# Issuing a pair's gate products before attention opens, a longer head norm in the issue model, and one tile of queries for the row scores

## The chip, the cores and the metric

One Trainium2 chip, one core. The metric is the device time of one execution in microseconds. Five engines are named throughout: PE (TensorE, matrix products, with PEld for its weight loads), DVE (VectorE), ACT (ScalarE), POOL (GpSimd) and SP (SyncE, which here only issues transfers). Each engine works through its own list of instructions in order and waits on semaphores for the others.

## The reference

One layer of a diffusion backbone. A normalised and modulated input goes through one projection `w_in`, whose columns feed a Fourier group and an attention group; both are gated by a SiLU and joined in one output projection:

```python
xn = _rms_norm(x, norm_g) * (1 + sc_x) + sh_x           # x: 1024 x 1024
fx_in, fx_gate, qx, kx, vx, nx_gate = split(xn @ w_in)   # 512 columns each
qx, kx = _rms_norm(heads(qx), q_norm_g), _rms_norm(heads(kx), k_norm_g)   # 8 heads of 64
f_out = fourier(fx_in, w_four) * silu(fx_gate)
s_loc = q . k over a 2-D neighbourhood, * 64 ** -0.5, + relative bias, masked
s_ctx = q . k over all 256 context tokens, * 64 ** -0.5
p = softmax(concat(s_loc, s_ctx))
na_out = (p_loc . v + p_ctx . v_ctx) * silu(nx_gate)
out = x + g_x * (concat(f_out, na_out) @ w_out)
```

Everything is float32.

## The kernel before

**Numbers.** Most products use a number format of PE with fewer mantissa bits (`R`). To keep float32's accuracy each operand is split in a high part and a low part, and three products (high by high, high by low, low by high) are summed. A split is a cast by ACT (`act.copy` into an `R` tile) and a subtraction by DVE or POOL (`tensor_tensor`, L198 or L110).

**Stages.** From 0 to some 128 us come the norm, the Fourier gate and the first part of the Fourier transform. Then one large stage runs, in which the projection, the context and the attention are interleaved, until some 498 us; after it stand the output products. Attention works on the eight heads as four pairs p of two heads h. For each pair:

- `project` (L810 on): eight row tiles t; for each, 24 products of 384 columns (`pqkv`, queries, keys and values of the pair at once), ACT copies the result to `raw`, and `head_norm` (L723 on) scales queries and keys: ACT squares, DVE sums (L729, L730), POOL takes the power -0.5 (`hrs`, L733), DVE multiplies (`raw`, L734).
- `gate_proj` (L843 on): 48 products of 512 columns (`png`), then ACT and DVE make the gate (L854, L855).
- `queries` (L898 on) and `keys`, each for two halves q of the 1024 rows: PE transposes four tiles of `raw` into a bank (`ptq`, L903; `ptk`, L917); ACT and DVE write high and low parts.
- `row_max` (L1158 on), once for each head and row tile: four score products (`s`, L1171 and L1173), DVE adds the bias and takes the maximum (`pr`, L1179), ACT the exponential (L1183).
- `probs` (L1240 on), twelve steps a head: PE transposes `pr` into a bank (`st`), ACT and DVE split it (`eh`, `el`), PE multiplies by the values (`pv`).

The last pair has the output products of the Fourier half (`po`, L1447) as its filler, and the splitting of their weights (`owr`, `oh`, `ol`) and inputs (`mh`, `ml`) beside it.

**How the scores keep the low parts.** Of a head h, `a` is its half of the 128 partitions (`HALF[h]`) and `b` the other. `qs1[h]` holds the high part of the transposed queries in `a` and the low part in `b`. `ks1[h]` holds the high part of the keys in `a` and again in `b`; `ks2[h]` their low part in `a` and zeros in `b`. So `qs1` by `ks1` is high by high plus low by high, in one product over 128 partitions. The missing high by low comes from `qs2[h]` (the high part copied to `a`, zeros in `b`) by `ks2[h]`.

**What sets the order.** The program writes each engine's list itself (`manual_schedule`). A small model of the engines runs while the program is built: `chain` hands each operation to an engine with a duration in us (`a_t`, `d_t`, `p_t` or a number), and an operation is written on its engine's list when the model says that it is free and the inputs are ready. PE's list is made from a set of generators, asked in turn (`seq_build`, `seq_rows`, `seq_scores` and others); only if none of them has work does `run_fill` take the next product of `feed`, which is the projection, then the gate products, then the output products. So a wrong duration costs no time in the model, but puts work on a list too early or too late. Operations with two possible engines (`split_by`, `copy_by`) go to the one that is free first in the model. `open_attention` (L963 on) allocates the attention's tiles, once the context is done; it lets POOL clear tiles and DVE build small constants, and counts that with `OP` us for POOL and `OD` us for DVE. `seq_build` calls it before the first `queries`. `PRB` and `EHB` are numbers of buffers for `pr` and for `eh` and `el`.

Of the kernel before, what the change touches and what calls it, by code (L numbers as in the profile page):

```python
# [26 lines left out]
AHEAD, GAINS = 2, ((0,), (1, 2), (3, 4), (5, 6), (7,), (), (), ())  # L27
S = dict(sem=0.13, rw=4, wo=2.6, rt=0, ri=12, rf=0, ro=1, ns=3, rr=2, rv=2)
WHO = dict(ml=(1, 0), ol=(0, 1), w=None, cw=(0, 1), ga=None, ce=(1, 0), el=(0,), vl=(0, 1), q2=(0,), kb=(0, 2), fm=None, wc=(2,), ec=(2,), oc=(0, 2), mc=(2, 0), cc=(2, 0), vc=(2,), fe=(0,), gc=(2,))
OP, OD, OC = 4.5, 2.0, 8.0  # L30
SEQ = 1024
CTX = 256
NB = 8
# [9 lines left out]
def tile_hybrid_block(  # L43
# [140 lines left out]
    def a_t(n):  # L184
        return 0.09 + n * 0.00083
# [624 lines left out]
    def project(p):  # L810
        raws[p] = []
        for t in range(NB):
            while now[0] < banks[0]:
                yield None
            if t % 4 == 0:
                while p and not has(("v", p - 1, 0, t // 4), ("v", p - 1, 1, t // 4)):
                    yield None
                raw = rawp.tile([P, 4, 384], F32, tag="raw", name="raw")
                raws[p].append(raw)
            o = pj("pqkv")[:, 0:384]  # L820
            ts_ = slice(t * P, (t + 1) * P)
            for k in range(KT):
                while ("w", p, k) not in done:
                    yield None
                wh, wl = weights[p][k]
                for n, (x, w) in enumerate(((xnh, wh), (xnh, wl), (xnl, wh))):
                    mm(o, x[k][:, ts_], w, start=(k == 0 and n == 0), stop=(k == KT - 1 and n == 2))  # L827
                    yield 0.16
                if t == NB - 1 and p < 3:
                    prep(p + 1, k)  # L830
            rt = raw[:, t % 4]
            sqt = rawp.tile([P, 256], F32, tag="sqt", name="sqt")
            while t > 1 and ("raw", p, t - 2) not in done:
                yield None
            banks.append(1e9)
            banks.pop(0)
            n1, n2, n3, n4 = head_norm(rt[:, 0:256], sqt, 4)
            chain((ACT_, a_t(384), lambda rt=rt, o=o: act.copy(rt, o), 0),  # L838
                  lambda: banks.__setitem__(0 if banks[0] == 1e9 else 1, clock()),
                  (ACT_, a_t(256), n1), (DVE_, 0.42, n2), (POOL_, 0.96, n3), (DVE_, d_t(256), n4),  # L840
                  lambda t=t: done.__setitem__(("raw", p, t), 1), rank=S["rr"])

    def gate_proj(p):  # L843
# [54 lines left out]
    def queries(p, q):  # L898
        cs = slice(512 * q, 512 * q + 512)
        tbs[0] -= 1  # L900
        pq = tb("ptq")
        for j in range(4):
            pe.transpose(pq[:, j * P:(j + 1) * P], raws[p][q][:, j, 0:P], ident)  # L903
        for h in range(2):
            a, b = HALF[h], HALF[1 - h]
            chain((ACT_, a_t(512), lambda h=h, a=a: act.copy(qs1[h][a, cs], pq[a])),
                  (DVE_, d_t(512), lambda h=h, a=a, b=b: dve.tensor_tensor(out=qs1[h][b, cs], in0=pq[a], in1=f(qs1[h][a, cs]), op=ALU.subtract)),
                  lambda h=h: give() if h else None,
                  copy_by(512, WHO["q2"], qs2[h][a, cs], f(qs1[h][a, cs])),
                  lambda h=h: done.__setitem__(("q", p, h, q), 1), rank=h)  # L910

    def keys(p, c, cs, srcs):
# [44 lines left out]


    gts, att = ExitStack(), ExitStack()
    gtp = ap1 = ap2 = qs1 = qs2 = ks1 = ks2 = eye = rrow = sel = biases = trs = sms = None  # L960
    PRB, VSB = 5, 1

    def open_attention():  # L963
        nonlocal gtp, ap1, ap2, qs1, qs2, ks1, ks2, eye, rrow, sel, biases, trs, sms
        gfs.close()
        pqs.close()
        gst.close()
        gtp = gts.enter_context(tc.tile_pool(name="gtp", bufs=1, **LT))
        ap1 = att.enter_context(tc.tile_pool(name="ap1", bufs=1, **LT))
        ap2 = att.enter_context(tc.tile_pool(name="ap2", bufs=2, **LT))  # L970
        qs1 = [ap1.tile([P, SEQ], R, name=f"qs1{h}") for h in range(2)]
        qs2 = [ap1.tile([P, SEQ], R, name=f"qs2{h}") for h in range(2)]
        ks1 = [ap1.tile([P, SEQ + CTX], R, name=f"ks1{h}") for h in range(2)]
        ks2 = [ap1.tile([P, SEQ + CTX], R, name=f"ks2{h}") for h in range(2)]
        for h in range(2):
            b = HALF[1 - h]
            pool.memset(f(qs2[h])[b], 0.0)
            pool.memset(f(ks2[h])[b], 0.0)
        eye = ap1.tile([104, 8], F32, name="eye")
        dve.tensor_copy(eye, ident[0:104, 0:8])  # L980
        for r in (32, 64, 96):
            dve.tensor_copy(eye[r:r + 8], ident[0:8, 0:8])
        rrow = [ap1.tile([104, P], R, name=f"rrow{n}") for n in range(2)]
        for r in rrow:
            dve.memset(f(r), 0.0)
        half = ap1.tile([104, 2], F32, name="half")
        sel = [ap1.tile([104, P], R, name=f"sel{z}") for z in range(2)]
        for z in range(2):
            dve.reduce_sum(half[:, z:z + 1], eye[:, 4 * z:4 * z + 4], axis=AX.X)
            dve.memset(f(sel[z]), 0.0)  # L990
            for h in range(2):
                r = slice(64 * h, 64 * h + 40)
                dve.tensor_copy(sel[z][r, HALF[h]], half[r, z:z + 1].broadcast_to([40, 64]))
        dve.tensor_tensor(out=eye[:, 0:4], in0=eye[:, 0:4], in1=eye[:, 4:8], op=ALU.add)
        biases = [ap1.tile([P, 896], F32, name=f"bias{n}") for n in range(2)]
        for b in biases:
            pool.memset(b[:, 256:512], 0.0)
        trs = [ap1.tile([P, 40], F32, name=f"tr{h}") for h in range(2)]
        sms = [ap1.tile([P, 8], F32, name=f"sm{h}") for h in range(2)]
        for h in range(2):  # L1000
            pool.memset(trs[h], 0.0)
        free[POOL_] = max(free[POOL_], now[0]) + OP
        free[DVE_] = max(free[DVE_], now[0]) + OD
        for e in (POOL_, DVE_):
            at(free[e], lambda e=e: issue(e))
        done["open"] = 1
# [151 lines left out]
    def row_max(p, h, t):  # L1158
# [8 lines left out]
        for z in range(2):  # L1167
            for o, kk in ((sl, lk), (sc, slice(SEQ, SEQ + CTX))):
                st, sp = (z == 0 and not (edge and o is sc)), (z == 1 and not (edge and o is sl))
                if z == 0:  # L1170
                    mm(o, qs1[h][:, ts_], ks1[h][:, kk], start=st, stop=sp)  # L1171
                else:
                    mm(o, qs2[h][:, ts_], ks2[h][:, kk], start=st, stop=sp)  # L1173
        now[0] += 2 * (nl + CTX) / 2400
        done["s", p, h, t] = 1
        pr = prs[p, h, t] = ap1.tile([P, 640], F32, tag="pr", bufs=PRB, name="pr")[:, 0:nl + CTX]
# [41 lines left out]


    STEPS = (10, 11, 0, 1, 2, 3, 12, 4, 13, 5, 6, 7)  # L1220
    EHB = 3
    pvs = {}

    def turned(p, h, t, kt):
# [324 lines left out]
    def feed():  # L1549
# [3 lines left out]
        for p in range(4):  # L1553
            yield from project(p)
            if p == 3:
                wst.close()
                yield from gate_rows()
                side.append(out_loads())
            while "open" not in done:
                yield None  # L1560
            yield from gate_proj(p)
            if p < 3:
                prep_gate(p + 1)
# [192 lines left out]
```

## Time and profile before

| | |
|---|---|
| three runs, us | 574.51, 576.97, 578.93 |
| median, us | 576.97 |
| profiled execution, us | 575.37 |
| its span, first to last instruction, us | 573.6 |
| PE, DVE, ACT, POOL busy, share of the span | 95%, 68%, 55%, 24% |
| granted PE clock, mean | 0.997 of 2.4 GHz |

A row of the timeline gives the start in us from the first instruction, the duration, the engine, the source line, the operation, what it writes and reads, and how many like it were merged; in brackets stands how long the engine was idle before it and what ended that. A product's recorded duration overlaps the next one's, so what a product costs is read from the distance between starts, or from the chain of work, which counts each moment once.

### The profile page before, as it was taken

Reading aid. Unit: us, or ns where it says so; the run is one execution under the profiler, and the core shown is the slowest. Engines: PE = TensorE matmul, PEld = TensorE weight load, DVE = VectorE, ACT = ScalarE, POOL = GpSimd, SP = SyncE. Lnnn points to the kernel's source line nnn. Section 1 sums busy time; section 2 is a strip of 40 time slices with the busy share of each in tenths; the row PEclk is TensorE's granted clock in tenths of the full one; section 3 lists DMA queues with packets and bytes.
Section 4 is the critical chain, followed back from the end, with each engine's and each line's share of the span. In section 5 each row is a group of like instructions: output and inputs, shape, how many; then the busy total and the mean of one; then the engine's idle time right before and its main releaser. Section 6 shows DMA issues by size and latency. Waiting matters only on the chain.

```text
span 573.6 us, 9000 instructions
## 1 busy us (share of the span) xinstructions
PE 546.6 (95%) x3299; PEld 483.5 (84%) x3299; DVE 388.5 (68%) x801; ACT 312.6 (55%) x662; POOL 139.9 (24%) x144
## 2 busy tenths in 40 slices
PE   4899999999999899999999999999999898989997
PEld 3677896799878889999989999899998687868886
DVE  5774756686754868866678667777765978783142
ACT  6865462355665368764688646767456855520000
POOL 2200000115702533112431032411224513540000
PEclk9999999999999899999999999999999999999999
DMA  8991046426551521110221111220113556120052
GB/s 339 412 408 58 1 148 215 152 89 198 193 147 38 179 65 42 42 43 37 81 66 45 30 49 51 70 70 1 42 46 112 184 191 203 73 92 0 1 201 93
DMA packets 41459, 64.64 MB, mean 113 GB/s; under 512 B 3268, under 2 KB 25156, under 8 KB 40392
## 3 DMA queue, kind: packets, MB, share of 16 engines
q1 hardware_dynamic: 40408, 60.40, 31.1%
q0 software_dynamic: 1008, 3.67, 1.9%
q8 instruction: 26, 0.43, 0.3%
q14 instruction: 17, 0.14, 0.1%
HBM read 55.15 MB, written 8.91 MB: 112 GB/s over the span
## 4 chain that ended last, share of the span: by engine, by line
PE 75%; DVE 8%; ACT 6%; DMA 6%; issue 2%; POOL 2%; SPq 1%; POOLq 0%; DVEq 0%; ACTq 0%
PE pqkv L827 20%; PE of L1623 8%; PE pg L365 7%; PE po L1447 5%; PE st L1251 4%; PE png L849 4%; DMA wr<-in_w_in_dram 3%; PE s L1171 2%; PE s L1173 2%; PE pv L1285 2%; PE pv L1275 2%; DMA x<-in_xb_dram 2%; DMA owr<-in_w_out_dram 2%; PE pc L1133 1%; PE pw L502 1%
## 5 line engine op out<-in xcount | busy, mean ns | idle before, releaser
L827 PE MATMUL pqkv<-wl,xnh 128*128 128x384 f32 x256 | 88.3, 345 | 0.0
L827 PE MATMUL pqkv<-wh,xnl 128*128 128x384 f32 x256 | 88.0, 344 | 0.0
L827 PE MATMUL pqkv<-wh,xnh 128*128 128x384 f32 x256 | 87.8, 343 | 0.0
L733 POOL TENSOR_TENSOR hrs<-hss,mhalf 128x4 f32<-128x4 f32 (+1 forms) x34 | 36.7, 1082 | 149.2 <-DVE hss L730 145.8
L1262 DVE TENSOR_TENSOR el<-st,eh 128x512 fp32r<-128x512 f32 (+2 forms) x96 | 53.5, 572 | 17.0 <-ACT eh L1261 16.3
L1261 ACT CAST eh<-st 128x512 fp32r<-128x512 f32 (+2 forms) x96 | 47.0, 494 | 29.4 <-PE st L1251 25.9
L1183 ACT ACTIVATE pr<-pr,tr 128x640 f32<-128x640 f32 (+1 forms) x64 | 51.5, 805 | 15.4 <-DVE tr L1179 15.1
L1179 DVE CUSTOM_DVE_ANT_0 pr<-s,bias 128x640 f32<-128x640 f32 (+1 forms) x64 | 50.2, 784 | 10.6 <-PE s L1173 10.2
L827 PEld LDWEIGHTS pqkv<-wh,xnh 128*128 128x128 f32 x256 | 48.7, 190 | 0.6
L827 PEld LDWEIGHTS pqkv<-wl,xnh 128*128 128x128 f32 x256 | 48.6, 190 | 0.5
L827 PEld LDWEIGHTS pqkv<-wh,xnl 128*128 128x128 f32 x256 | 48.6, 190 | 0.4
L1251 PE MATMUL st<-ident,pr 128*128 128x128 f32 x304 | 47.3, 272 | 0.1
L1251 PEld LDWEIGHTS st<-ident,pr 128*128 128x128 f32 x304 | 37.0, 140 | 2.8 <-DVE el L1262 0.5
L1447 PE MATMUL po<-oh,mh 128*128 128x512 f32 x88 | 31.0, 396 | 3.0 <-DVE y L1453 1.5
L1627 DVE TENSOR_TENSOR y<-y,of 128x512 f32<-128x512 f32 (+1 forms) x17 | 11.1, 656 | 32.3 <-PE of L1623 32.3
L1171 PE MATMUL s<-ks,qs 128*128 128x256 f32 (+1 forms) x128 | 29.9, 313 | 0.7 <-DVE tr L1179 0.7
L203 ACT CAST wh<-wr 128x384 fp32r<-128x384 f32 (+1 forms) x44 | 22.6, 539 | 12.7 <-DMA wr<-in_w_in_dram 10.6
L1173 PE MATMUL s<-ks,qs 128*128 128x256 f32 (+1 forms) x128 | 28.3, 302 | 0.0
L198 DVE TENSOR_TENSOR wl<-wr,wh 128x384 fp32r<-128x384 f32 (+1 forms) x29 | 21.5, 754 | 9.6 <-ACT wh L203 7.7
L198 POOL TENSOR_TENSOR wl<-wr,wh 128x384 fp32r<-128x384 f32 (+1 forms) x19 | 20.9, 1104 | 28.9 <-ACT wh L203 15.2
L365 PE MATMUL pg<-xnh,w 128*128 128x512 f32 x96 | 27.3, 406 | 0.0
L838 ACT COPY raw<-pqkv 128x384 f32<-128x384 f32 x32 | 15.3, 478 | 21.4 <-PE pqkv L827 21.1
(295 smaller groups left out, 1442.9 us busy)
## 6 DMA issues: line engine op xcount, KB each, us to landing
wd<-in_w_ada_b_dram SPq DMA_DIRECT2D x8, 1024.0 KB, 11.6
wr<-in_w_in_dram SPq DMA_DIRECT2D x40, 192.0 KB, 2.8
wr<-in_w_in_dram SPq DMA_DIRECT2D x24, 256.0 KB, 3.1
x<-in_xb_dram SPq DMA_DIRECT2D x8, 512.0 KB, 7.3
wdg<-in_w_ada_g_dram SPq DMA_DIRECT2D x8, 512.0 KB, 4.7
owr<-in_w_out_dram SPq DMA_DIRECT2D x16, 256.0 KB, 3.4
y<-in_xb_dram SPq DMA_DIRECT2D x8, 512.0 KB, 5.4
out_dram<-y SPq DMA_DIRECT2D x15, 256.0 KB, 2.1
```

The source lines that it names most:

```text
L198: return [(e, time(n), lambda eng=eng: eng.tensor_tensor(out=out, in0=in0, in1=in1, op=op)) for e, eng, time in (both[k] for k in who)]
L365: mm(pg[j][hf], wj, x[i][:, hs], start=(i == 0 and g == 0), stop=(i == KT - 1 and g == 2))
L827: mm(o, x[k][:, ts_], w, start=(k == 0 and n == 0), stop=(k == KT - 1 and n == 2))
L1171: mm(o, qs1[h][:, ts_], ks1[h][:, kk], start=st, stop=sp)
L1173: mm(o, qs2[h][:, ts_], ks2[h][:, kk], start=st, stop=sp)
L1179: dve.tensor_tensor_reduce(out=pr, in0=sv, in1=bt, scale=-1.0, scalar=3.0e38, op0=ALU.add, op1=ALU.min, accum_out=tr[:, t:t + 1])
L1183: (ACT_, a_t(nl + CTX) + 0.15, lambda: act.activation(pr, pr, AF.Exp, bias=tr[:, t:t + 1], scale=-1.0, accum_out=sm[:, t:t + 1]), 1),
L1251: pe.transpose(s[:, j * P:(j + 1) * P], turned(p, h, t, kt), ident)
L1261: chain((ACT_, a_t(m), lambda: act.copy(eh[:, w], s3)), (DVE_, d_t(m), lambda: dve.tensor_tensor(out=el[:, w], in0=s3, in1=f(eh)[:, w], op ...
L1262: (DVE_, d_t(m), lambda: dve.tensor_tensor(out=el[:, w], in0=s3, in1=f(eh)[:, w], op=ALU.subtract)), give,
L1447: mm(o, mf[k][m][:, ts_], wf[hf][k][w_], start=(k == 0 and n == 0), stop=(k == 3 and n == 2))
L1623: mm(o[:, cs], ma[k][m][:, ts_], w[:, cs], start=(k == 0 and n == 0), stop=(k == 3 and n == 2))
```

## The change

Five edits. (1) `feed` no longer waits for `open_attention` before the gate products of a pair. (2) In `project` the model's duration of POOL's power goes from 0.96 to 1.1 us and that of DVE's multiplication from 0.34 (`d_t(256)`) to 0.9 us. (3) The second score products read `qs1` instead of `qs2`: `ks2` is zero in `b`, so the low part of the queries that stands there in `qs1` is multiplied by zero. `qs2`, its sixteen copies and its two clearings go. (4) `PRB` goes from 5 to 6 and `EHB` from 3 to 4. (5) `OP` goes from 4.5 to 3.5 us.

```diff
-OP, OD, OC = 4.5, 2.0, 8.0
+OP, OD, OC = 3.5, 2.0, 8.0
@@ project
-                  (ACT_, a_t(256), n1), (DVE_, 0.42, n2), (POOL_, 0.96, n3), (DVE_, d_t(256), n4),
+                  (ACT_, a_t(256), n1), (DVE_, 0.42, n2), (POOL_, 1.1, n3), (DVE_, 0.9, n4),
@@ queries
                   lambda h=h: give() if h else None,
-                  copy_by(512, WHO["q2"], qs2[h][a, cs], f(qs1[h][a, cs])),
                   lambda h=h: done.__setitem__(("q", p, h, q), 1), rank=h)
@@
-    PRB, VSB = 5, 1
+    PRB, VSB = 6, 1
@@ open_attention
-        qs2 = [ap1.tile([P, SEQ], R, name=f"qs2{h}") for h in range(2)]
...
-            pool.memset(f(qs2[h])[b], 0.0)
             pool.memset(f(ks2[h])[b], 0.0)
@@ row_max
-                if z == 0:
-                    mm(o, qs1[h][:, ts_], ks1[h][:, kk], start=st, stop=sp)
-                else:
-                    mm(o, qs2[h][:, ts_], ks2[h][:, kk], start=st, stop=sp)
+                mm(o, qs1[h][:, ts_], (ks1, ks2)[z][h][:, kk], start=st, stop=sp)
@@
-    EHB = 3
+    EHB = 4
@@ feed
-            while "open" not in done:
-                yield None
             yield from gate_proj(p)
```

The edits move rows on all engines. On POOL, at the opening of attention (`hrs` is the power of the head norm, `bias` and `tr` are tiles of the row scores), before:

```order
L733 TENSOR_TENSOR hrs<-hss,mhalf 128x4
L977 MEMSET qs_2102 64x1024
L978 MEMSET ks_2106 64x1280
L977 MEMSET qs_2103 64x1024
L978 MEMSET ks_2107 64x1280
L997 MEMSET bias_2133 128x256
L997 MEMSET bias_2134 128x256
```

and now:

```order
L733 TENSOR_TENSOR hrs<-hss,mhalf 128x4
L975 MEMSET ks_2104 64x1280
L975 MEMSET ks_2105 64x1280
L994 MEMSET bias_2129 128x256
L994 MEMSET bias_2130 128x256
```

The two clearings of `qs2` are gone and the rest follows sooner. DVE's list at the same place keeps its order. On PE, at the first transposes of the queries (first pair, first half), before:

```order
L827 MATMUL pqkv<-wh,xnh_406 128x384
L827 MATMUL pqkv<-wl,xnh_406 128x384
L827 MATMUL pqkv<-wh,xnl_410 128x384
L903 MATMUL ptq<-ident,raw 128x128 x4
L917 MATMUL ptk<-ident,raw 128x128 x4
```

and now:

```order
L827 MATMUL pqkv<-wh,xnh_406 128x384
L827 MATMUL pqkv<-wl,xnh_406 128x384
L827 MATMUL pqkv<-wh,xnl_410 128x384
L827 MATMUL pqkv<-wh,xnh_407 128x384
L827 MATMUL pqkv<-wl,xnh_407 128x384
L827 MATMUL pqkv<-wh,xnl_411 128x384
L903 MATMUL ptq<-ident,raw 128x128 x4
L916 MATMUL ptk<-ident,raw 128x128 x4
```

Three projection products have moved ahead of the transposes. In both kernels 51 more of them follow, then the context's key transposes and, before, six projection products (now three), and only then the first gate product. On PE, at the second half's transposes in the last pair (`pgr` turns the output gate's column into rows), before:

```order
L827 MATMUL pqkv<-wh,xnl_413 128x384
L1380 MATMUL pgr<-ident,gcol 128x128 x8
L849 MATMUL png<-xnh_121,gh 128x512
L849 MATMUL png<-xnl_125,gh 128x512
L849 MATMUL png<-xnh_121,gl 128x512
L903 MATMUL ptq<-ident,raw 128x128 x4
```

and now:

```order
L827 MATMUL pqkv<-wh,xnl_413 128x384
L1374 MATMUL pgr<-ident,gcol 128x128 x8
L849 MATMUL png<-xnh_121,gh 128x512
L849 MATMUL png<-xnl_125,gh 128x512
L849 MATMUL png<-xnh_121,gl 128x512
L849 MATMUL png<-xnh_121,gh 128x512
L849 MATMUL png<-xnl_125,gh 128x512
L849 MATMUL png<-xnh_121,gl 128x512
L849 MATMUL png<-xnh_122,gh 128x512
L903 MATMUL ptq<-ident,raw 128x128 x4
```

Four gate products have moved ahead of the transposes. At the same half in the first pair 18 gate products stand ahead of `ptq` where 15 stood. In the last pair, between these transposes and the end of attention, DVE's list loses two casts of `qs`, one split of context values, two of values and one of a mix tile (`ml`), and gains two casts and two splits of output weights; POOL's changes the other way for the splits. On SP three loads change places with a neighbour: a bias tile with a weight tile, `y1` with a bias tile, `y6` with an output weight.

## Rows read from the trace of the kernel before

**Rows 1.** The page: span, and PE's busy time, share, instructions.

```profile
span 573.6 us, 9000 instructions
PE 546.6 (95%) x3299; PEld 483.5 (84%) x3299; DVE 388.5 (68%) x801; ACT 312.6 (55%) x662; POOL 139.9 (24%) x144
```

**Rows 2.** Stretches: length, each engine's busy time (instructions), granted clock, DMA share, GB/s.

```profile
190.00:200.00 10.00, 7.63 (x38) 7.36 (x37) 7.92 (x23) 3.77 (x7) 4.09 (x8) 0.83 0.58 165
200.00:430.00 230.00, 229.04 (x1458) 218.57 (x1457) 170.90 (x384) 153.25 (x345) 59.76 (x64) 1.00 0.16 49
430.00:507.00 77.00, 69.58 (x402) 59.29 (x400) 62.14 (x113) 46.17 (x92) 30.83 (x22) 1.00 0.42 146
...
194.30:197.70 3.40, 3.40 (x14) 3.40 (x13) 2.58 (x7) 1.85 (x3) 1.01 (x1) 0.50 0.53 146
440.00:460.00 20.00, 16.97 (x93) 13.81 (x93) 18.79 (x32) 16.70 (x34) 10.38 (x7) 1.00 0.53 185
```

**Rows 3.** Waits of PE: who for whom, us in total, times, longest.

```profile
PE ptq L903 <- DVE raw L734: 3.8, 2, 2.4
PE pv L1275 <- DVE el L1262: 2.9, 4, 1.2
```

**Rows 4.** Timeline of PE at the first transposes of the queries.

```profile
191.19 0.49 PE L903 MATMUL ptq<-ident,raw 128*128 128x128 f32 x3
194.05 0.33 PE L903 MATMUL ptq<-ident,raw 128*128 128x128 f32 x1 [2.37 <-DVE raw L734]
195.31 0.52 PE L827 MATMUL pqkv<-wl,xnh 128*128 128x384 f32 x1
```

**Rows 5.** The chain that ended last: start, us, engine, what, how many.

```profile
188.19 2.10 DVE eye L982
190.30 0.99 DVE eye L982
...
280.91 2.43 PE pqkv L827 x14
283.34 3.91 PE png L849 x17
```

**Rows 6.** Timeline of DVE: the raw behind the first and the last transposes.

```profile
193.57 0.42 DVE L734 TENSOR_TENSOR raw<-raw,hrs 128x256 f32<-128x256 f32 x1
...
436.10 1.48 DVE L734 TENSOR_TENSOR raw<-raw,hrs 128x256 f32<-128x256 f32 x1 [1.18 <-POOL hrs L733]
```

**Rows 7.** Line 982 alone: duration in ns as least, median, most.

```profile
L982 DVE COPY eye<-ident x3: 160/989/2098, 188.0 to 190.3; 8x8 f32<-8x8 f32 x3
```

**Rows 8.** Timeline of POOL at the opening of attention.

```profile
188.21 0.95 POOL L977 MEMSET qs<- 64x1024 f32 x1
189.10 1.17 POOL L978 MEMSET ks<- 64x1280 f32 x1
...
192.35 0.65 POOL L997 MEMSET bias<- 128x256 f32 x2
```

**Rows 9.** Groups of DVE by form: count, busy us, mean ns, idle before.

```profile
L203 DVE CAST qs<-qs 64x512 fp32r<-64x512 f32 x16 | 7.0, 441 | 0.1
```

**Rows 10.** Timeline of PE in the last pair: rows that follow a pause.

```profile
437.63 0.33 PE L903 MATMUL ptq<-ident,raw 128*128 128x128 f32 x1 [1.42 <-DVE raw L734]
...
449.56 0.39 PE L1275 MATMUL pv<-el,vs 128*128 128x256 f32 x1 [1.13 <-DVE el L1262]
...
459.50 0.50 PE L1447 MATMUL po<-oh,mh 128*128 128x512 f32 x1 [1.46 <-DVE gate L855]
...
476.10 0.38 PE L1275 MATMUL pv<-el,vs 128*128 128x256 f32 x1 [1.20 <-DVE el L1262]
```

**Rows 11.** Timeline of PE at the second transposes of the first pair.

```profile
211.09 0.92 PE L903 MATMUL ptq<-ident,raw 128*128 128x128 f32 x4
211.85 0.60 PE L917 MATMUL ptk<-ident,raw 128*128 128x128 f32 x4
212.20 0.49 PE L849 MATMUL png<-xnh,gh 128*128 128x512 f32 x1
```

**Rows 12.** Timeline of POOL behind the last pair's head norm.

```profile
436.03 2.68 POOL L1360 TENSOR_TENSOR owr<-owr,grow 128x512 f32<-128x512 f32 x2
```

More of the change, by code (lines that the diff above doesn't have):

```diff
@@ L959, in tile_hybrid_block @@
     gts, att = ExitStack(), ExitStack()
-    gtp = ap1 = ap2 = qs1 = qs2 = ks1 = ks2 = eye = rrow = sel = biases = trs = sms = None
-    PRB, VSB = 5, 1
+    gtp = ap1 = ap2 = qs1 = ks1 = ks2 = eye = rrow = sel = biases = trs = sms = None
+    PRB, VSB = 6, 1
     def open_attention():
-        nonlocal gtp, ap1, ap2, qs1, qs2, ks1, ks2, eye, rrow, sel, biases, trs, sms
+        nonlocal gtp, ap1, ap2, qs1, ks1, ks2, eye, rrow, sel, biases, trs, sms
         gfs.close()
```

## The prediction

> **What bounds the kernel now.** I read the head of the page first: TensorE (PE) is busy for 95% of a span of 573.6 us [rows 1]. So an engine that gets lighter gives nothing by itself; only PE's idle time, its time at the lower clock, or PE work that goes away can be won. The change takes no matrix product away (3299 [rows 1]; the order lists as many rows on PE with the change as without). The table by stretch then says where PE is idle [rows 2]: 2.37 us in 190 to 200, 0.96 in the 230 us from 200 to 430, 7.42 in 430 to 507. The losses before 180 us and after 507 us lie where the two orders agree or nearly so. The list of PE's waits names the largest of the rest [rows 3]: the transposes of the queries (ptq) wait for DVE's scaled rows (raw), 3.8 us in two places; the probability products (pv) wait for el, 2.9 us in four places.
>
> The rows of PE around the first ptq show the first place whole [rows 4]: three transposes go at 191.19, the fourth waits 2.37 us and goes at 194.05. Behind it the products stand at 1.2 GHz: the granted clock of 194.3 to 197.7 is 0.50 [rows 2], where a 384-column product normally costs 2.43/14 = 0.174 us and a 512-column one 3.91/17 = 0.23 us [rows 5]. So this stall costs 2.4 us of waiting and 0.50 x 3.4 = 1.7 us of clock.
>
> Why raw was late is in DVE's and POOL's rows. DVE works through the opening of attention before the raw at 193.57 [rows 6]. Two copies of eight by eight numbers take 2.10 and 0.99 us there [rows 5], though the line's shortest took 0.16 [rows 7]. POOL clears qs and ks in turn in just that time, 0.95 us each for qs and 1.17 for ks [rows 8]; the first of the long copies (188.19 + 2.10 = 190.29) ends with the first ks clearing (189.10 + 1.17 = 190.27), the second (191.29) with the second qs clearing. So DVE's copies were held by POOL's clearings. The Trainium skill (SBUF — State Buffer, SBUF: two separate sides) says that the port pair which these two engines share is an exclusive lock for a whole instruction; this trace agrees, with 2.10 us against 0.16.
>
> **The change part by part.**
>
> *The wait for "open" ahead of the gate products: 0.* The first ptq is written after attention opens, and in both kernels it stands ahead of the last 54 to 57 projection products of the first pair, which stand ahead of that pair's gate products. The wait was already over when it was reached. It would cost or bring something only if attention opened after the first projection.
>
> *Row scores with one tile of queries.* Sixteen DVE casts go, 7.0 us in all [rows 9], and two clearings of qs on POOL. The products read qs1 instead, as many and as wide: 0 on PE. The casts lie beside PE's work; were that cover gone, they would be worth up to 7.0 us. The two clearings are worth something at the opening. DVE's second copy is now let go after one or two ks clearings (189.4 or 190.5), the third after the next instruction of POOL, so by 190.5 to 191.15 instead of 191.29; and the later cast that a fourth clearing held up for some 0.4 us runs freely. Together 0.5 to 1.2 us; I take 0.9. The clearings of bias (0.65 us [rows 8]) still stand beside the copies, so I do not take more.
>
> *The longer head norm in the issue model (1.1 and 0.9 us instead of 0.96 and 0.34).* It changes no duration; the planner believes raw to be later and puts more products ahead of what needs it.
> - First ptq: three more 384-column products, 3 x 0.174 = 0.5 us of the wait filled. What is left of it is 2.37 - 0.5 - 0.9 = 1.0 us.
> - The clock: the pauses of 1.13 to 1.46 us in the last pair [rows 10] were followed by no drop (granted 1.00 in 430 to 507 [rows 2]). So I take it that a pause of 1.0 us causes none, and the 1.7 us come back. Bounds 0 and 1.7.
> - Second ptq of the first pair: its four transposes last 0.76 us to the next group, which takes 0.35 us for four [rows 11], so 0.4 us of hidden wait. Now 18 gate products instead of 15 stand between the projection's end and it, 0.7 us more: 0.4 us won.
> - Second ptq of the last pair: PE waits 1.42 us [rows 10] for a raw that took 1.48 us on DVE, against 0.42 for the same operation at 193.57 [rows 6], while POOL multiplied output weights from 436.03 on [rows 12]. Seven gate products instead of three stand ahead, 4 x 0.23 = 0.9 us. POOL's order is the same there, so the raw itself stays as slow: 0.9 us won, bounds 0 and 1.4.
> - Behind the later ptq stand ACT's and DVE's copies of queries and keys, and behind these the first scores. PE has gate and projection products in between, 229.04 us of 230 busy [rows 2]; a microsecond's delay is hidden there.
>
> *One buffer more for pr (6) and for eh, el (4), and POOL free 1 us earlier in the model.* No instruction more. They let rows run further ahead and reorder DVE, ACT and POOL in all four pairs. The middle has 0.96 us to give, so 0 there. On SP only three loads swap places with a neighbour (a bias tile past a weight tile, y1 past a bias tile, y6 past an output weight), one place each on a queue that PE's list of waits does not name among its largest: 0. In the last pair DVE gets two weight splits more and hands value splits and a mix split to POOL. The three further waits of PE there (1.13, 1.46 and 1.20 [rows 10]) I leave as they are: bounds 3 us less and 6 us more, below.
>
> **Sum.** 0.9 + 0.5 + 1.7 + 0.4 + 0.9 = 4.4 us. The profiled execution's own time is 575.4 us, its span 573.6 and 1.8 around it; that gives 571.0. It lies 1.6 us below the median of the three runs, 576.97, so against the median I forecast **572.6 us**.
>
> **The rivals.**
> - *The clock falls all the same.* The pause shrinks but 1.2 GHz is still granted for 3.4 us. For it: only one pause this long with a drop is in the trace, so nothing shows where the edge lies. Against it: four shorter ones without. Gain 2.7 us: 574.3. The Trainium skill (TensorE: Matmul & The Clock Gate, What's actually happening) says that the monitor which grants the clock runs free of the kernel. By that rule the same pause may cost clock in one run and not in the next; the one drop here neither supports nor refutes that.
> - *The last pair's waits go too.* DVE is busy 18.79 of 20 us in 440 to 460 [rows 2], and it loses two casts of queries there; with four eh and el buffers more work stands between a transpose and its product. If three of the waits of 1.1 to 1.5 us mostly vanish, 3 us more: 569.6.
> - *Slower: POOL's new work blocks DVE in the last pair.* The raw beside a two-operand instruction of POOL took 1.06 us more [rows 6, 12], and the splits that move to POOL are of that kind. If six of DVE's splits and casts there lose 1.06 us each, that is 6.4 us on an engine with 1.2 us to spare, and el, gate and y are late by it: 579.0. It ends slower than before when more than four of them are so held (4.4/1.06). Against it: before, several were held already, and DVE's own list is a little shorter now.
> - *The change does nothing.* True of the gate wait; for the rest the order shows the rows moved.
>
> **Chances.** Forecast 0.47 (own range 571 to 574.5), clock falls 0.20, last pair's waits go 0.18, slower 0.10, something else 0.05. The range from 568.5 to 577.5 holds the first three and the milder part of the fourth. A measurement of this kernel can tell about 1% (5.8 us, the bound being 571.2) from no change. Faster by more than that: most of the third case and the lower edge of the first, 0.27. Slower by over 1%: the worst of the fourth and of the rest, 0.05. Within 1%: 0.68.
>
> **What would show it.** In the new trace: the eye copies end by 191.2 and raw starts by 193.1; the wait of the first ptq is 0.6 to 1.3 us; 190 to 200 has a granted clock of 1.00; the last ptq waits about 0.5 us; 430 to 507 has 6 to 7 us of idle PE. I am wrong if PE's idle time in the middle grows over 2 us (the new order leaves less room than the old), or if el and y are later in the last pair.

## The result, and the profile after

The changed kernel takes **569.6 us** (median; 569.40 to 570.55) against 576.94 (574.51 to 578.93): the ratio is 0.987, with an interval of 0.984 to 0.990. That is 7.3 us or 1.3% faster. The time lies in the stated range, but below the forecast's own range of 571 to 574.5 us: the gain is 2.9 us larger than the 4.4 us of the sum, and on the far side of the 1% bound, to which I had given a chance of 0.27.

The head of the page after, as in [rows 1]:

```profile
span 567.7 us, 8971 instructions
PE 545.2 (96%) x3299; PEld 483.9 (85%) x3299; DVE 377.5 (67%) x788; ACT 311.9 (55%) x659; POOL 139.5 (25%) x142
```

The table by stretch of after, with the columns of [rows 2] (the granted clock is the first number behind POOL's) and one stretch more at 18.7:

```profile
18.70:22.10 3.40, 3.40 (x17) 3.40 (x16) 2.65 (x5) 2.69 (x6) 1.29 (x2) 0.50 1.03 419
190.00:200.00 10.00, 9.32 (x57) 9.06 (x56) 8.61 (x24) 5.37 (x10) 4.01 (x7) 1.00 0.78 239
200.00:430.00 230.00, 230.00 (x1477) 221.51 (x1477) 162.89 (x378) 154.69 (x348) 60.30 (x63) 1.00 0.17 49
430.00:507.00 77.00, 72.66 (x404) 61.01 (x403) 64.50 (x110) 43.69 (x87) 34.14 (x25) 1.00 0.44 151
440.00:460.00 20.00, 16.54 (x95) 13.44 (x94) 17.63 (x31) 13.33 (x30) 10.69 (x7) 1.00 0.42 136
```

Idle time of PE goes from 2.37 to 0.68 us in 190 to 200, from 0.96 to 0 in the middle, and from 7.42 to 4.34 in 430 to 507. The last of these is not a like comparison: after is some 4 us further on in its list there, and a wait of 1.13 us for `y` lies behind 507. Counted between the marks C and D (below), in the columns of [rows 2], before and after,

```profile
433.13:526.13 93.00, 85.58 (x465) 71.97 (x465) 71.08 (x120) 47.88 (x94) 36.88 (x26) 1.00 0.39 132
429.00:520.48 91.48, 86.01 (x465) 71.88 (x465) 71.01 (x118) 46.94 (x92) 39.50 (x28) 1.00 0.39 134
```

it goes from 7.42 to 5.47 us. So idle time falls by 1.7, 1.0 and 2.0 us, 4.6 in all. The granted clock is 1.00 at the first transposes now; but this execution was granted 0.50 from 18.7 to 22.1, where the two orders agree.

The waits of PE in after that answer to [rows 3]:

```profile
PE ptq L903 <- DVE raw L734: 1.0, 2, 0.7
PE pv L1279 <- DVE el L1256: 1.2, 1, 1.2
PE pv L1269 <- DVE el L1256: 1.0, 1, 1.0
PE s L1167 <- DVE tr L1173: 1.5, 3, 1.0
```

The timeline of PE in after, at the first `ptq` and in the last pair, which answers to [rows 4, 10]:

```profile
193.56 0.49 PE L903 MATMUL ptq<-ident,raw 128*128 128x128 f32 x3
194.72 0.33 PE L903 MATMUL ptq<-ident,raw 128*128 128x128 f32 x1 [0.68 <-DVE raw L734]
...
433.52 0.33 PE L903 MATMUL ptq<-ident,raw 128*128 128x128 f32 x1 [0.36 <-DVE raw L734]
...
446.42 0.39 PE L1269 MATMUL pv<-el,vs 128*128 128x256 f32 x1 [1.03 <-DVE el L1256]
...
452.57 0.45 PE L1279 MATMUL pv<-el,vs 128*128 128x384 f32 x1 [1.16 <-DVE el L1256]
...
454.31 0.74 PE L1167 MATMUL s<-ks,qs 128*128 128x256 f32 x4 [0.96 <-DVE tr L1173]
...
512.18 0.50 PE L1441 MATMUL po<-oh,mh 128*128 128x512 f32 x1 [1.13 <-DVE y L1447]
```

The waits for raw fall from 3.8 to 1.0 us in all. Two waits of `pv` are left of four, both in the last pair, which had two before as well (1.13 and 1.20 us, now 1.03 and 1.16). The scores' waits for the row maximum grow, from 0.7 us in two places to 1.5 in three.

**Where the time went.** Busy time hides short waits, since the rows of neighbouring products overlap. So I use four marks on PE that all kernels pass in the same order, and take the time between them. A is the start of the last six products of `pc` (ahead of the opening), B the last projection product `pqkv` of the first pair, C the first `pgr` of the last pair, D the first `of` (behind attention). B in the timeline of before, and C (433.1) in its rows of the tile `pgr`:

```profile
206.22 0.35 PE L827 MATMUL pqkv<-wh,xnl 128*128 128x384 f32 x1
L1380 PE MATMUL pgr<-ident,gcol x16: 272/275/275, 433.1 to 434.8; 128*128 128x128 f32 x16
```

The same two views of after:

```profile
204.75 0.33 PE L827 MATMUL pqkv<-wh,xnl 128*128 128x384 f32 x1
L1374 PE MATMUL pgr<-ident,gcol x16: 272/275/275, 429.0 to 430.7; 128*128 128x128 f32 x16
```

Between these, 226.9 and 224.25 us, lie 1439 products in either kernel. The table has all kernels of this study, read in the same way from their profiled executions. The last column says where the rows show a granted clock of 0.50 (but for the tail after PE's work); each such place is 3.4 us long, in e2's last pair 6.8.

| kernel | A to B | B to C | C to D | granted clock 0.50 from |
|---|---|---|---|---|
| before | 26.83 | 226.91 | 93.00 | 194.3 |
| after | 23.53 | 224.25 | 91.48 | 18.7 |
| e1 scores | 24.05 | 226.79 | 91.45 | none |
| e2 norm | 24.49 | 225.79 | 94.81 | 19.0, 100.9, 455.9 |
| e3 scores, norm | 23.54 | 225.47 | 91.10 | 18.3, 448.4 |
| e4 scores, buffers | 24.06 | 226.11 | 91.12 | none |
| e5 clearings back | 24.61 | 224.25 | 92.77 | 454.5 |
| e6 late constants | 22.61 | 225.14 | 92.22 | 19.0, 100.9, 455.9 |
| e7 before, late constants | 22.62 | 230.42 | 93.11 | 99.9, 209.1 |
| e8 = e3 with casts | 23.54 | 226.65 | 91.50 | 19.9, 101.8 |
| e9 before, ScalarE copies | 24.26 | 226.79 | 92.98 | none |
| e10 after, ScalarE copies | 22.62 | 224.22 | 91.47 | 101.6 |
| e11 = e12 with casts | 23.52 | 226.17 | 91.36 | none |
| e12 = after, EHB 3 | 23.52 | 224.25 | 92.75 | 17.9, 454.8 |

After against before: 3.3 us won from A to B, 2.7 from B to C, 1.5 from C to D, 7.5 in all. A itself comes 1.8 us later in after (181.22 against 179.39 us), with the stretch at 18.7 ahead of it; executions with no such stretch ahead of A reach it at 179.4 to 180.2. Behind D after is 0.2 us shorter. 7.5 - 1.8 + 0.2 = 5.9, the difference of the spans, 573.6 - 567.7.

How well do such distances repeat? After, e5, e10 and e12 have one and the same list on PE, and their distances from B to C lie within 0.03 us; those of before and e9 within 0.12. From C to D e5 and e12 take 1.3 us more than after: they have a stretch at 0.50 there and after has none.

**The medians.** One such stretch in a run costs at most 3.4 x 0.5 = 1.7 us (1.3 from C to D, as above) and lowers the run's mean granted clock by 0.003. So the mean clock of a timed run shows about how many there were. The 49 runs of before beside the experiments, sorted by it:

| mean clock | runs | median, us |
|---|---|---|
| 1.000 | 5 | 574.12 |
| 0.996, 0.997 | 9 | 575.94 |
| 0.994 | 27 | 576.99 |
| 0.991 | 5 | 578.74 |
| 0.988 | 3 | 579.60 |

After's four had 0.996, 0.997, 0.996 and 0.993. So the profiled execution of before, with one stretch, was a quick one, and its median has two; after's median has one. At a like clock the gain is 6.4 to 6.5 us (569.48 at 0.996 and 0.997 against 575.94; 570.55 at 0.993 against 576.99 at 0.994); the rest of the 7.3 us goes with the number of stretches. A mean of 1.000 leaves no room for such a stretch, so in five runs of before the clock was not low at the first transposes either, though the order that makes PE wait there is the same.

### The profile page after: what moved, and what is told of

It is laid out like the page before. It is cut to its first block, busy times and chain, and to the rows that moved or that the text cites. A ratio compares the mean times of both kernels' runs of the same rounds, so it can differ in the third digit from the quotient of the medians.

```text
span 567.7 us, 8971 instructions
## 1 busy us (share of the span) xinstructions
PE 545.2 (96%) x3299; PEld 483.9 (85%) x3299; DVE 377.5 (67%) x788; ACT 311.9 (55%) x659; POOL 139.5 (25%) x142
## 4 chain that ended last, share of the span: by engine, by line
PE 82%; DVE 6%; DMA 3%; ACT 3%; POOL 3%; issue 2%; SPq 1%; POOLq 0%; ACTq 0%; DVEq 0%
PE pqkv L827 20%; PE of L1615 8%; PE pg L365 7%; PE s L1167 6%; PE png L849 6%; PE st L1245 6%; PE po L1441 5%; PE pv L1279 3%; PE pv L1269 3%; DMA x<-in_xb_dram 2%; PE pc L1130 1%; PE pw L502 1%; PE ada L284 1%; DMA wr<-in_w_in_dram 1%; PE pgs L284 1%
## 5 line engine op out<-in xcount | busy, mean ns | idle before, releaser
L827 PE MATMUL pqkv<-wh,xnl 128*128 128x384 f32 x256 | 86.8, 339 | 0.0
L1256 DVE TENSOR_TENSOR el<-st,eh 128x512 fp32r<-128x512 f32 (+2 forms) x96 | 53.9, 574 | 19.9 <-ACT eh L1255 19.3
L1167 PE MATMUL s<-ks,qs 128*128 128x256 f32 (+1 forms) x256 | 48.0, 309 | 1.5 <-DVE tr L1173 1.5
L1167 PEld LDWEIGHTS s<-ks,qs 128*128 128x128 f32 x256 | 39.5, 188 | 4.3 <-DVE tr L1173 3.3
L1615 PE MATMUL of<-ol,mh 128*128 128x512 f32 (+1 forms) x68 | 25.6, 377 | 0.0
```

The costliest lines, as they stand in the source:

```text
L1167: mm(o, qs1[h][:, ts_], (ks1, ks2)[z][h][:, kk], start=st, stop=sp)
L1256: (DVE_, d_t(m), lambda: dve.tensor_tensor(out=el[:, w], in0=s3, in1=f(eh)[:, w], op=ALU.subtract)), give,
L1615: mm(o[:, cs], ma[k][m][:, ts_], w[:, cs], start=(k == 0 and n == 0), stop=(k == 3 and n == 2))
```

## The experiments

Each of the three sets, e1 to e4, e5 to e8 and e9 to e12, was measured beside its own runs of the kernel before, whose medians were 577.47, 576.33 and 576.91 us.

### One part at a time: e1 to e4

e1 has the scores' edit alone (edit 3), e2 the head norm's numbers alone (edit 2), e3 everything but the buffer counts (so `OP` at 3.5 too), e4 everything but the head norm's numbers.

```diff
e1, against after
-  ... (POOL_, 1.1, n3), (DVE_, 0.9, n4),
+  ... (POOL_, 0.96, n3), (DVE_, d_t(256), n4),
-    PRB, VSB = 6, 1
+    PRB, VSB = 5, 1
-    EHB = 4
+    EHB = 3
-OP, OD, OC = 3.5, 2.0, 8.0
+OP, OD, OC = 4.5, 2.0, 8.0
+            while "open" not in done:
+                yield None
e2, against before
-  ... (POOL_, 0.96, n3), (DVE_, d_t(256), n4),
+  ... (POOL_, 1.1, n3), (DVE_, 0.9, n4),
e3, against after: PRB 5, EHB 3
e4, against after: (POOL_, 0.96, n3), (DVE_, d_t(256), n4)
```

> The kernel before with the score edit alone (no qs2, its sixteen copies or its two clearings; PRB 5, EHB 3, OP 4.5 and the old head norm numbers). Theory: the two clearings are worth 0.9 us at the opening of attention, the first wait of ptq falls from 2.4 to about 1.4 us, and a pause of that length costs no clock, so 1.7 us more come back: 577.0 - 2.6 = 574.3 us, granted clock 1.00 around 195 us. Rival, the clock falls at 1.4 us all the same: about 576. Rival, the sixteen copies are what counts (they free DVE in the last pair): 572 or less with the idle time of 430 to 507 under 6 us.

> The kernel before with the longer head norm alone (1.1 and 0.9 us). Theory: three products more ahead of the first ptq, so its wait falls from 2.4 to 1.9 us; 0.4 us at the second ptq of the first pair and 0.9 at that of the last pair: 1.8 us less, 575.2, if the clock still falls after a pause of 1.9 us; 573.5 if it does not. Rival, the longer numbers are what removes the waits of the last pair (later products there meet finished work): 572 or less.

> The changed kernel with PRB 5 and EHB 3, so scores and head norm without the buffers. Theory, the 4.4 us of the sum are theirs and the further 3 us (the middle's 0.96 us of idle PE and some 2 us in the last pair) belong to the buffers: 572.6. Rival, the buffers are worth nothing and casts and head norm brought everything: 569.6. If it is under 569, the buffers cost.

> The changed kernel with the old head norm numbers (0.96 and 0.34), so scores and buffers. Its lists are row for row those of the change with OP at 4.5 as well, so OP moves nothing here. Theory, the head norm is worth 0.5 + 0.4 + 0.9 = 1.8 us and nothing else: 571.4. Rival, the head norm also orders the last pair better: 573 to 574. Rival, it brings nothing beside the buffers: 569.6.

Measured: e1 571.59 us (ratio 0.9896, 0.9855 to 0.9937), e2 576.12 (0.9956, 0.9921 to 0.9991), e3 569.48 (0.9861, 0.9817 to 0.9904), e4 572.34 (0.9908, 0.9874 to 0.9942).

What follows. By the medians the scores' edit alone wins 5.9 us, where 2.6 stood in the sum, and the head norm's numbers alone 1.35. The clock is part of both. Three of e1's four runs had no stretch at 0.50, where the median of before has two; against the runs of before at 1.000 (574.12) e1 (571.4 to 571.8) is 2.5 us faster, and the table has 2.8, 0.1 and 1.55 us for it, 1.7 of them the stretch at 194.3. Of e2's ten runs, five had four such stretches (0.988); its two at 0.997 (571.28, 572.63) are 3 to 5 us faster than the median of before at that clock. So it isn't shown that one of the two edits carries the change.

e4 and the changed kernel differ by the head norm's numbers alone. By the medians these bring 2.7 us (572.34 to 569.6), where 1.8 stood; by the table they bring it elsewhere: 0.5 from A to B as forecast, 1.9 instead of 0.4 from B to C, and from C to D 0.4 lost instead of 0.9 won. (e1 and e3, which differ in `OP` too, have 0.5, 1.3 and 0.35, the last with a stretch at 0.50 in e3.)

e3 and the changed kernel differ by the buffers alone. By the medians these bring nothing (569.48 and 569.6), but the table splits that: 1.2 us are won from B to C, where the sum had 0, and 0.4 lost from C to D, though there e3 has a stretch at 0.50 and after has none.

Of the theories written ahead, those of e2 and e4 lie within the measured intervals. e1 came out under its 574.3 us, at the number of the rival that the copies count, though 2.8 us of it came at the opening, as the theory had it; e3 came out at the number of its rival, that the buffers are worth nothing.

e2 gains little by its median also since a new wait opens in its last pair. The timeline of PE in e2:

```profile
457.21 0.90 PE L1171 MATMUL s<-ks,qs 128*128 128x384 f32 x2 [4.52 <-DVE tr L1179]
```

DVE in e2 just ahead of it:

```profile
451.35 1.78 DVE L198 TENSOR_TENSOR ol<-owr,oh 128x512 fp32r<-128x512 f32 x1
453.06 3.36 DVE L198 TENSOR_TENSOR ml<-omr,mh 128x1024 fp32r<-128x1024 f32 x1
456.34 0.81 DVE L1179 CUSTOM_DVE_ANT_0 pr<-s,bias 128x640 f32<-128x640 f32 x1
```

POOL in e2 at the same time:

```profile
451.25 1.33 POOL L198 TENSOR_TENSOR ol<-owr,oh 128x512 fp32r<-128x512 f32 x1 [0.71 <-ACT oh L203]
452.84 2.50 POOL L198 TENSOR_TENSOR ml<-omr,mh 128x1024 fp32r<-128x1024 f32 x1 [0.25 <-ACT mh L203]
```

And the stretch of e2 around the wait, in the columns of [rows 2]:

```profile
455.90:462.70 6.80, 5.49 (x20) 5.09 (x21) 4.77 (x10) 2.81 (x6) 0.00 (x0) 0.50 0.01 2
```

Two of DVE's splits run beside two of POOL's, the row maximum behind them is late, and PE waits 4.52 us for its buffer; then the granted clock is 0.50 for 6.8 us. This is the mechanism of the "slower" rival, in another kernel than the one it was forecast for. In after, splits and casts there are held too (`mh` 2.14 us beside POOL's `ml` of 2.43), but PE's longest wait is 1.16 us.

### The opening: e5, e6, e7, e9, e10

e5 puts two clearings of 64x1024 back on POOL. e6 and e7 write DVE's opening constants (the eye copies, `rrow`, `half`, `sel`) some ten rows later, in after and in before. e9 and e10 put the four eye copies on ScalarE, in before and in after.

```diff
e5, against after
+            pool.memset(f(ks2[h])[b][:, 0:SEQ], 0.0)
             pool.memset(f(ks2[h])[b], 0.0)
e6 against after, e7 against before
-        dve.tensor_copy(eye, ident[0:104, 0:8])
...
+        at(clock() + 7.0, constants)
e9 against before, e10 against after
-        dve.tensor_copy(eye, ident[0:104, 0:8])
+        act.copy(eye, ident[0:104, 0:8])
-            dve.tensor_copy(eye[r:r + 8], ident[0:8, 0:8])
+            act.copy(eye[r:r + 8], ident[0:8, 0:8])
```

> The changed kernel with two clearings of 64 x 1024 put back on POOL at the opening of attention (the same part of ks2 cleared twice); every list is else row for row that of the change. Theory, DVE's copies of the eye wait for POOL's clearings: raw 0.6 to 1.2 us later, the first wait of ptq 1.3 to 1.9 us instead of 0.7, the granted clock stays 1.00 as it did after 1.6 us with the head norm alone: 570.5. Rival, the clearings do not hold DVE: 569.6 and a wait of 0.7. Rival, the clock falls: 572.2.

> The changed kernel with DVE's constants of the opening (eye, rrow, half, sel) written eight rows later on DVE's list, behind the raw and the splits of the first queries and keys; all other lists are the same. Theory, what is left of the first wait goes: ptq waits 0 instead of 0.7 us: 568.9. Rival, the constants then hold up the next raw or the first scores behind them: 569.6 or more, with a new wait of PE between 196 and 215 us.

> The kernel before with nothing but DVE's constants written ten rows later, behind the first raw and the splits of the first queries and keys. Theory, the first stall cost 2.4 us of waiting and 1.7 us of clock: the wait goes, the granted clock stays 1.00 and the time is 4.1 us less than before: 573.0. Rival, the clock falls for another reason: 574.7 with 0.50 still granted for 3.4 us there. Rival, the wait moves on to the first scores: 576 or more.

> The kernel before, with one edit: the four eye copies of the opening of attention stand on ScalarE instead of VectorE, where they are beside POOL's clearings. All five lists are otherwise those of before. This run asks why the late constants brought the kernel before nothing: there the first ptq no longer waited, but the key copies behind the moved constants were 2.35 us late for the first scores, and the clock fell after that. Theory (the stall at the first ptq is worth its 2.4 us of waiting and 1.7 us of clock, as long as VectorE's work is not merely put later): VectorE has 3.4 us less ahead of raw, nothing of it stands later, so PE has no wait over 0.5 us between 186 and 212 us, and the time is 576.9 - 4.1 = 572.8 us, 572 to 574. Rival (the order of before takes back whatever is won at its first ptq, at the first scores or later): 575.5 or more, with a new wait of 1 us or longer before 215 us. Rival (the clock falls in any case): 574.5.

> The changed kernel with the same single edit: the four eye copies on ScalarE, the lists otherwise those of the changed kernel. What is left of the wait at its first ptq is 0.68 us. Theory: that wait goes and nothing comes back, 569.6 - 0.7 = 568.9 us. Rival (ScalarE's four copies push its own queue, which makes the squares of the head norm and the copies of queries and keys, later): 569.6 or more.

Measured: e5 571.07 us (0.9909, 0.9885 to 0.9933), e6 569.24 (0.9880, 0.9859 to 0.9902), e7 576.74 (0.9995, 0.9975 to 1.0015), e9 575.68 (0.9976, 0.9958 to 0.9995), e10 569.23 (0.9862, 0.9839 to 0.9886).

e5: the first `ptq` waits 1.77 us instead of 0.68, so the two clearings are worth 1.1 us, where the sum had 0.9; the clock stays at 1.00 there. PE's timeline in e5:

```profile
194.70 0.33 PE L903 MATMUL ptq<-ident,raw 128*128 128x128 f32 x1 [1.77 <-DVE raw L734]
```

e9 missed: 572.8 us was expected, and its time lies at the 575.5 or more of its rival, that the order of before takes back what is won, though without the new wait that this rival names. Its first `ptq` still waits, although the eye copies no longer stand on DVE. PE in e9:

```profile
193.83 0.33 PE L903 MATMUL ptq<-ident,raw 128*128 128x128 f32 x1 [1.38 <-DVE raw L734]
```

DVE in e9 ahead of it:

```profile
188.62 0.30 DVE L985 MEMSET rrow<- 104x128 f32 x2
188.84 0.10 DVE L989 TENSOR_REDUCE half<-eye 104x1 f32<-104x4 f32 x1
188.92 0.17 DVE L990 MEMSET sel<- 104x128 f32 x1
189.12 1.99 DVE L993 CAST sel<-half 40x64 fp32r<-40x64 f32 x2
191.12 0.16 DVE L989 TENSOR_REDUCE half<-eye 104x1 f32<-104x4 f32 x1
191.26 0.17 DVE L990 MEMSET sel<- 104x128 f32 x1
191.46 1.80 DVE L993 CAST sel<-half 40x64 fp32r<-40x64 f32 x2
193.28 0.16 DVE L994 TENSOR_TENSOR eye<-eye 104x4 f32<-104x4 f32 x1
```

POOL in e9 at the same time:

```profile
188.95 0.95 POOL L977 MEMSET qs<- 64x1024 f32 x1
189.84 1.22 POOL L978 MEMSET ks<- 64x1280 f32 x1
191.11 0.95 POOL L977 MEMSET qs<- 64x1024 f32 x1
192.01 1.20 POOL L978 MEMSET ks<- 64x1280 f32 x1
```

The casts behind the copies are now held by POOL's clearings in their place: 1.99 and 1.80 us, until the first and the second clearing of `ks` end, where a pair of them takes 0.39 in after. Taking the held instructions away moves the hold to the next ones. Of the wait 1.0 us is won, and this execution lost no clock at all; the medians differ by 1.2.

e7 missed too, and shows where a repaired stall can come out again. Its first `ptq` does not wait; but the first scores do, and the clock falls behind them. PE in e7:

```profile
208.61 0.36 PE L1174 MATMUL s<-ks,qs 128*128 128x256 f32 x1 [2.35 <-DVE ks L203]
```

The stretch of e7 behind that, in the columns of [rows 2]:

```profile
209.10:212.50 3.40, 3.40 (x11) 2.81 (x11) 1.53 (x5) 2.61 (x4) 2.30 (x2) 0.50 0.36 108
```

The constants, now at 198.7 to 201.2, push the raw rows and, behind them, the key copies (207.18 to 208.46 on DVE). A to B is 4.2 us shorter and B to C 3.5 longer. e6 does the same on a smaller scale: 0.9 won ahead of B, 0.9 given back behind it. So in this place the wait is that of a chain (raw, copies of queries and keys, scores), and a delay of DVE shows at the next link if it does not at the first. e6's median, 569.24, lies between its theory (568.9) and its rival (569.6). e10 removes what was left of the first wait without moving anything later, though there too the first pair of casts is held (2.26 us): A to B is 0.9 us shorter and the rest as in after. At 569.23 it is the lowest median of the study, but its interval and that of the changed kernel overlap, so it is not shown to be faster.

### The casts: e8, e11, e12

e8 is e3, and e11 the changed kernel (with EHB 3), with sixteen casts of 64x512 put back on DVE; nothing reads what they write. e12 is the changed kernel with EHB 3, whose lists are row for row those of the changed kernel, and the base of e11.

```diff
e11, against e12
+                  lambda h=h, a=a: dve.tensor_copy(dq[0][a], f(qs1[h][a, cs])),
                   lambda h=h, a=a: done.__setitem__(("q", p, h, q), 1), rank=h)
...
+        dq.append(ap1.tile([P, 512], R, name="dq"))
e12, against after
-    EHB = 4
+    EHB = 3
```

> Scores and head norm (PRB 5, EHB 3) with sixteen casts of 64 x 512 put back on DVE, into a tile that nothing reads; every list is else row for row that of scores and head norm alone (569.5 us). Theory, the casts delay DVE's raws, splits and maxima behind which PE waits in the last pair: 570.5 to 571, the waits of pv and s from 430 on longer by about 1 us. Rival, not the casts but the reordered lists brought the last pair's gain: 569.5.

> The changed kernel with sixteen casts of 64x512 put back on VectorE in the places where those of before stood; they write a tile that nothing reads. EHB is 3, so that the tile has room; all five lists are otherwise those of the changed kernel, and those of the next kernel, which has EHB 3 without the casts. Theory of the prediction (the casts lie beside PE's work): 569.6, the same as the next one within 0.5 us. Rival (between 200 and 430 us PE waits for VectorE in many pieces too short to show as idle, so VectorE's 7 us are partly on the path): 571.2 to 572.6; an earlier kernel of this study with them lost 1.6 us by its trace and 3.0 us by medians of different calls, and here both stand beside one run of the kernel before.

> The changed kernel with EHB 3 instead of 4; its five lists are row for row those of the changed kernel. Prediction's reading (one buffer more of eh and el brings nothing): 569.6, as the changed kernel. Rival (el is released too late with three buffers, and pv waits for it): 570.5 or more, with longer waits of pv for el. It is also the base of the kernel before it in this call.

Measured: e8 572.45 us (0.9931, 0.9909 to 0.9953), e11 570.39 (0.9889, 0.9865 to 0.9913), e12 569.97 (0.9884, 0.9860 to 0.9909).

The medians of e11 and e12 differ by only 0.4 us, which alone would say that the casts are free. But the mean granted clock of e11's runs was 0.996 to 1.000, and that of e12's 0.990 to 1.000. At 1.000, e11 took 570.11 and 570.39 (and 569.50 at 0.999) and e12 569.19; at 0.996 and 0.997, e11 571.43 and 571.93 and e12 569.40 and 569.52. So at a like clock e11 is 0.3 to 2.5 us slower, which is too wide for a price. The traces tell more: from B to C e11 takes 226.2 us and e12 224.3. B and C in e12, as above:

```profile
204.42 0.34 PE L827 MATMUL pqkv<-wh,xnl 128*128 128x384 f32 x1
L1374 PE MATMUL pgr<-ident,gcol x16: 272/275/275, 428.7 to 430.3; 128*128 128x128 f32 x16
```

B and C in e11:

```profile
203.64 0.34 PE L827 MATMUL pqkv<-wh,xnl 128*128 128x384 f32 x1
L1377 PE MATMUL pgr<-ident,gcol x16: 272/275/275, 429.8 to 431.5; 128*128 128x128 f32 x16
```

All 1.9 us of it arise in five steps of 0.3 to 0.5 us, each at the products of a row score: two wait for the row maximum on DVE, and three for ACT's last copy of the keys, which follows DVE's work on them. The first is this wait, for the row maximum on DVE, in the timeline of PE in e11; in e12 the same scores go at 217.49 without one:

```profile
217.26 0.86 PE L1170 MATMUL s<-ks,qs 128*128 128x384 f32 x4 [0.43 <-DVE tr L1176]
```

So the casts are not hidden in the middle: about 1.9 us of their 7.1 are on the path. e8 against e3 has 1.2 us from B to C and 0.4 from C to D, where only e3 has a stretch at 0.50, and 3.0 by the medians of two sets, more than its theory had. That the casts explain all of the middle's gain is not shown: e1, without casts, was no quicker there than before (226.79 against 226.91), in a list that is ordered otherwise. What the casts cost hangs on the order around them.

That e12 is as fast as after, within what can be told (569.97 and 569.6, and 224.25 us from B to C in both), shows that the fourth buffer of `eh` and `el` brings nothing. So what e3 and the changed kernel differ by is the sixth buffer of `pr`. `OP` alone was not tried; its share of the changed kernel's gain is open.

## Why the prediction was right and wrong

- **The wait for "open": 0.** Right. With it put back, the order has the same rows on all five engines.
- **The first stall: right, term by term, in the profiled executions.** Predicted 0.9 + 0.5 + 1.7 = 3.1 us; A to B is 3.3 shorter. The two clearings measured 1.1 (e5), the three projections 0.5 (after against e4, which differ by the head norm's numbers alone), and what is left is 0.68 us where I said 1.0. The eye copies ended at 192.4 and raw started at 194.25, later than the 191.2 and 193.1 that I named; but A is 1.8 us later in after, and counted from A both are 0.6 us or more ahead of what I said. The eye copies took 2.59 us instead of 3.27, as POOL cleared only `ks`. DVE in after, where [rows 5, 6] show before:

```profile
189.84 2.59 DVE L979 COPY eye<-ident 8x8 f32<-8x8 f32 x3
...
194.25 0.42 DVE L734 TENSOR_TENSOR raw<-raw,hrs 128x256 f32<-128x256 f32 x1
```

POOL in after, where [rows 8] show before:

```profile
190.03 2.38 POOL L975 MEMSET ks<- 64x1280 f32 x2
```

- **"Clock falls all the same": not here.** At the first transposes pauses of 0.68, 1.38 and 1.77 us (after, e9, e5) were followed by a granted clock of 1.00. In these executions the bound of no drop was the right end; over many runs the 1.7 us are no constant, as five of 49 runs of before lost no clock at all.
- **"The middle has 0.96 us to give": the step that failed.** It gave 2.7 us, of which the sum had 0.4: on this ground it put the buffers at 0 there, which brought 1.2 (after against e3), and the head norm's numbers at 0.4, which brought 1.9 (after against e4; such shares depend on what else is in the kernel, and do not add up). I took PE's busy time in 200 to 430, 229.04 of 230, for the room that there was. But waits of a few tenths of a microsecond do not show in it: e11 loses 1.9 us from B to C against e12, and PE's idle time there is only 0.76 us larger. The room was to be read from the starts of products, not from their busy time.
- **"Behind the later ptq ... a microsecond's delay is hidden there", and the casts at 0: wrong.** The prediction named their price without cover, up to 7.0 us, and then took them for covered by the same busy share. About 1.9 us of them are on the path (e11).
- **The second `ptq` of the last pair: right at its place, but it does not reach D.** The wait went from 1.42 to 0.36 us with the raw as slow as before (1.50 us on DVE); I had said 0.5. But after against e4 shows nothing of it at D: 91.48 us from C to D against 91.12, neither with a stretch at 0.50.
- **"The three further waits I leave as they are": nearly right in sum, by luck.** From C to D PE's idle time fell by 2.0 us: 1.1 at `ptq`, 1.5 at `po`, which waited for `gate` and no longer does, and 0.2 at `pv` and at the waits for `y`, while the scores' waits for the row maximum took 0.8 more. (The sign that I named, 6 to 7 us of idle PE in 430 to 507, was missed with 4.34; 1.1 us more lie behind 507 in after.) Of the 2.0 us 1.5 were won in time. e1 has as much with the scores' edit alone (1.55), so it can come with two casts fewer and the order that goes with them. The rival "the last pair's waits go too" has the measured time, 569.6, but not its cause: it wanted 3 us more from there, and got 0.6; most of the rest came from the middle.
- **"POOL's new work blocks DVE": seen, but not slower.** The scores' waits for the row maximum grow by 0.8 us beside splits and casts that are held. e2 shows the mechanism with 4.5 us, when the head norm's numbers are changed without the scores' edit.
- **The buffers: 0.** Right for the whole kernel (e3, e12), but not for the reason given: the middle had room and gave 1.2 us, and the last pair lost 0.4 of it or more, as only e3 has a stretch at 0.50 there.
- **From the profile to the median.** I carried the sum over from one execution with one stretch at 0.50 to a median with two. At a like clock the gain is 6.4 to 6.5 us, not 7.3. The change of the median holds the stretch that went at 194.3 only on average, as other places (18, 100 and 455 us) take and give such stretches from run to run.

## What to carry to other kernels

A TensorE that is busy for 99.6% of a stretch can still lose 1% there: read how far apart the same products start, between marks that both orders pass, before calling an edit on another engine hidden. Work removed from an engine that feeds a chain can be worth something at each link of it, and how much depends on the order around it (1.9 us in one order, 0.1 in another); work only put later came out at the next link. A part that measures 0 by the median can be a gain in one stretch and a loss in the next. Count how often the granted clock is low before carrying one profile's time over to a median.

## What the runs showed of the hardware

- The same pauses were followed by a lower clock in one execution and not in another. After and e12 have the same lists and nearly the same waits in the last pair (in e12 1.15 and 0.97 us at 452.25 and 453.99); after is granted 1.00 there, e12 is not. The stretch of e12, in the columns of [rows 2]:

```profile
454.80:458.20 3.40, 3.40 (x9) 2.61 (x9) 2.22 (x8) 0.82 (x2) 0.00 (x0) 0.50 0.44 117
```

The Trainium skill (TensorE: Matmul & The Clock Gate, What's actually happening) says that the monitor which grants the clock runs free of the kernel; the prediction could not tell, and these two traces agree with it.

- POOL's clearings write zeros and read nothing, and yet hold DVE's copies of 8x8 and casts of 40x64 numbers. DVE's own reduction and clearing at 191.12 and 191.26 us in e9, beside POOL's clearing from 191.11 on, took 0.16 and 0.17 us; in after the same two, at 193.43 and 193.56 with no clearing beside them, took as long.
